# Rotary stage of a two-layer hybrid backbone: rotated result written to the tile of the rotated half and stored from there, context columns stored on their own

## Chip, cores, metric

The kernel runs as one program on one core of a Trainium2 chip. The metric is device microseconds (us) of one execution. A TensorE clock of 1.00 in the rows is 2.4 GHz, 0.50 is 1.2 GHz, and values between are a mix of the two over a stretch.

## The reference, cut to what matters

Two layers (l = 0, 1) run over 256 context tokens and 1024 latent tokens of width 1024. Each layer modulates the stream, applies one projection, splits its columns over three branches (a bidirectional RWKV-7 scan A, grouped-query attention B, neighbourhood attention C), gates them, projects back and normalises. The context is dropped after layer 0, so layer 1 needs no context queries.

The stage of this document prepares q and k of branch B. Each head is divided by its root mean square; latent tokens (not context tokens) are then rotated by position:

```python
def _apply_axial_rope(x, cos, sin):
    x1, x2, x3, x4 = jnp.split(x, 4, axis=-1)
    rotated = jnp.concatenate([-x2, x1, -x4, x3], axis=-1)
    return (x * cos[:, None] + rotated * sin[:, None]).astype(x.dtype)
...
gk_l = _apply_axial_rope(gk_l, cos, sin)
gq_l = _apply_axial_rope(gqa_q(aq_l), cos, sin)
gk_c, gv_c = gqa_kv(ak_c, av_c)
```

## The kernel before

Features lie on the 128 partitions, tokens on the columns: 256 context columns (`TC`), then 1024 latent ones (`TL`), 1280 in all (`T`). A feature block of 128 rows is one projection tile. Float32 products are split into high and low parts, three matmuls per 128 features (lines 203 to 205), into PSUM tiles of pool `pj` (3 buffers).

`layer_proj` runs the projections of a layer in order: RWKV inputs, two gate blocks, then four calls of `qk_proj` (k of both kv heads, then three q blocks of two heads each), the value projection (lines 415 to 417, matmuls into `pv`), and further on RWKV, the remaining projections and the attention.

`qk_proj` takes the PSUM blocks with ScalarE twice: squared into `sq` (line 347) and scaled into `raw` (line 348; the tile's name is `qr`). TensorE sums the squares (353), ScalarE and VectorE make the reciprocal root (354, 355), VectorE multiplies it into `raw` (356). Four DMAs copy the latent columns of `raw` with 32-partition groups swapped into `rot` (364); GpSimd multiplies `rot` by the sine and `raw` by the cosine (365, 366), VectorE adds (367), and one DMA stores to DRAM (368). `raw`, `sq` and `rot` each have two buffers. A new tile may be written only when everything that used the old tile in that buffer, DMAs included, has finished. For context columns `lo` is 0; in layer 1 only k has them, q calls have `lo` = 256.

All five engines run their own queue in order, and SyncE (SP) issues nearly all DMAs. The order within a queue is not the order of the code: a scheduler places each instruction by a simulated timeline when the kernel is built. So an edit in one stage can move instructions of others. This matters most in the stage in which the RWKV chain (waves of 4 steps; 40 steps per layer; line 724 is one product of each step, line 684 a merge, 713 and 734 the other products of the chain) and the attention (scores `st` of lines 963 and 964, running maximum 894 and 896, weighted values `y` 948) of a layer share the engines. They do not depend on each other; attention that is not done when the chain ends runs on alone.

Of the kernel before, what the change touches and what calls it, by code (L numbers as in the profile page):

```python
# [11 lines left out]
ALU = mybir.AluOpType  # L12
# [6 lines left out]
TC = 256  # L19
# [24 lines left out]
def body(tc, a):  # L44
    nc = tc.nc
# [136 lines left out]
    def layer_proj(l, hd, fw, lay, mid):  # L182
# [25 lines left out]
        def proj(m, evac, blocks=(0, 1, 2)):  # L208
            w = load_w(m)
            for b in blocks:  # L210
                block(w, b, evac)
# [58 lines left out]
        for c in range(3):  # L270
# [43 lines left out]
            for g in range(3):  # L314
                tts = range(4 * g, min(4 * g + 4, 10))
                pt = pq.tile([128, 4, 128], F32, tag="pq", name="pt")
                for j, tt in enumerate(tts):
# [6 lines left out]
                                  in_=vt[:, :n, :])  # L324
# [15 lines left out]
        def qk_proj(m, gcol, e, sc, dst, blocks):  # L340
            raw = sp.tile([128, T], F32, tag="qr", name="qr")
            sq = sp.tile([128, T], F32, tag="sq", name="sq")
            lo = 0 if 0 in blocks else TC

            def ev(b, ps):
                t0, n = BLK[b]
                nc.scalar.activation(out=sq[:, t0:t0 + n], in_=ps, func=AF.Square)
                nc.scalar.activation(out=raw[:, t0:t0 + n], in_=ps, func=AF.Copy, scale=gcol)  # L348
            proj(m, ev, blocks)
            for b in blocks:  # L350
                t0, n = BLK[b]
                ps = pq.tile([128, 512], F32, tag="pq", name="psn")
                nc.tensor.matmul(out=ps[:, :n], lhsT=bones, rhs=sq[:, t0:t0 + n], start=True, stop=True)
                nc.scalar.activation(out=sq[:, t0:t0 + n], in_=ps[:, :n], func=AF.Sqrt, scale=sc, bias=eps[:, e:e + 1])
            nc.vector.reciprocal(sq[:, lo:], sq[:, lo:])
            nc.vector.tensor_tensor(out=raw[:, lo:], in0=raw[:, lo:], in1=sq[:, lo:], op=ALU.mult)
            if not rope:
                for nm in ("cos", "sin"):
                    rope.append(sp.tile([128, TL], F32, tag=nm, name=nm, bufs=1))
                    nc.sync.dma_start(out=rope[-1], in_=a[nm])  # L360
            cos, sin = rope
            rot = sp.tile([128, TL], F32, tag="rot", name="rot")
            for q in range(4):
                nc.sync.dma_start(out=rot[32 * q:32 * q + 32, :], in_=raw[32 * (q ^ 1):32 * (q ^ 1) + 32, TC:T])
            nc.gpsimd.tensor_tensor(out=rot, in0=rot, in1=sin, op=ALU.mult)
            nc.gpsimd.tensor_tensor(out=raw[:, TC:], in0=raw[:, TC:], in1=cos, op=ALU.mult)
            nc.vector.tensor_tensor(out=raw[:, TC:], in0=raw[:, TC:], in1=rot, op=ALU.add)
            nc.sync.dma_start(out=dst[:, lo:], in_=raw[:, lo:])

        def store(dst, b, o):  # L370

# [26 lines left out]
        for i, m in list(enumerate(M_RG))[:2]:  # L398
            g_proj(m, gate_d[i], blks)
        qk_proj(M_AK, pp[:, l, PC_KN:PC_KN + 1], 1, 1.0 / 64, pair(k_d, 0), allb)  # L400
        qk_proj(M_AQ[0], pp[:, l, PC_QN:PC_QN + 1], 0, 1.0, pair(q_d, 0), blks)
        wvh = sp.tile([128, KT, 384], F32R, tag="wvh", name="wvh", bufs=1)
        wvl = sp.tile([128, KT, 384], F32R, tag="wvl", name="wvl", bufs=1)
# [5 lines left out]
        for i in (1, 2):  # L409
            qk_proj(M_AQ[i], pp[:, l, PC_QN:PC_QN + 1], 0, 1.0, pair(q_d, i), blks)  # L410
# [1018 lines left out]
```

## Time and profile before

| quantity | value |
|---|---|
| median of 3 runs | 2448.75 us (2443.36 to 2449.61) |
| profiled execution's own time | 2449.5 us |
| its span, first to last instruction | 2447.7 us |
| mean granted TensorE clock | 0.934 |
| busy: TensorE, VectorE, GpSimd, ScalarE | 90%, 66%, 48%, 41% |

In the rows below PE is TensorE, PEld its weight load, DVE VectorE, ACT ScalarE, POOL GpSimd, SP SyncE; PEq, SPq and so on are their queues. Matmuls overlap, so their starts tell the pace better than their durations do. An instruction with "[4.78 <-ACT qr L348]" behind it found its engine idle for 4.78 us before it, and the wait ended with that instruction. Line numbers are those of the kernel before; in the changed kernel what follows line 364 stands 2 lines later.

### The profile page before, as it was taken

To read this page: it belongs to the slowest core of one execution; us is meant where nothing else is said; L and a number is where in the kernel's file an instruction comes from. 1 tells how busy PE (TensorE), PEld (TensorE's weight loads), DVE (VectorE), ACT (ScalarE), POOL (GpSimd) and SP (SyncE) were. 2 spreads that over 40 slices of the span, in tenths; PEclk is the share of its full clock that TensorE was granted. 3 is DMA by queue.
4 is the path that set the end of the run, shared out by engine and by line. 5 is a ranking of instruction groups with operands and counts; after the bars stand their busy time and mean duration, and the time that the engine had idled before them with its cause. 6 is when DMAs were issued, how large, how long until landed. Compare 5 with 4: busy or idle time off the path is not lost. (4 is left out here: it accounts for less than half of the span.)

```text
span 2447.7 us, 57800 instructions
## 1 busy us (share of the span) xinstructions
PE 2206.0 (90%) x22616; PEld 1657.5 (68%) x22616; DVE 1615.7 (66%) x3063; ACT 1005.5 (41%) x2186; POOL 1180.5 (48%) x1438
## 2 busy tenths in 40 slices
PE   6999999997887898989999999899969888889897
PEld 3777898775555555555798777697746555556497
DVE  5687434445766878686387797524557788788746
ACT  3333413334544544454343443313345555545522
POOL 3465425424555555454155465533455565565453
PEclk9999999996887999989899999999968999999999
DMA  7344424527445544452233445335464545333342
GB/s 282 111 156 157 134 85 103 144 79 164 111 115 118 122 102 124 125 168 64 73 94 106 136 162 181 112 90 127 113 152 113 117 116 124 81 84 87 100 153 87
DMA packets 448241, 298.17 MB, mean 122 GB/s; under 512 B 249600, under 2 KB 395880, under 8 KB 446944
## 3 DMA queue, kind: packets, MB, share of 16 engines
q1 hardware_dynamic: 439936, 281.71, 41.9%
q0 software_dynamic: 7392, 10.28, 1.6%
q8 instruction: 178, 2.92, 0.5%
q10 hardware_dynamic: 640, 2.49, 0.4%
q14 instruction: 95, 0.78, 0.1%
HBM read 198.37 MB, written 91.79 MB: 119 GB/s over the span
## 5 line engine op out<-in xcount | busy, mean ns | idle before, releaser
L204 PE MATMUL pj<-hlo,wh 128*128 128x512 f32 (+1 forms) x1072 | 402.8, 376 | 13.1 <-DVE hlo L480 7.6
L203 PE MATMUL pj<-hhi,wh 128*128 128x512 f32 (+1 forms) x1072 | 403.2, 378 | 9.2 <-ACT qr L348 5.1
L205 PE MATMUL pj<-hhi,wl 128*128 128x512 f32 (+1 forms) x1072 | 402.0, 376 | 0.2 <-POOL wl L169 0.2
L204 PEld LDWEIGHTS pj<-hlo,wh 128*128 128x128 f32 x1072 | 205.7, 192 | 55.6 <-DVE hlo L480 7.7
L203 PEld LDWEIGHTS pj<-hhi,wh 128*128 128x128 f32 x1072 | 204.8, 192 | 54.3 <-issue 6.8
L169 POOL TENSOR_TENSOR wl<-wf,wh 128x512 fp32r<-128x512 f32 x104 | 142.9, 1379 | 202.7 <-ACT wh L168 185.4
L205 PEld LDWEIGHTS pj<-hhi,wl 128*128 128x128 f32 x1072 | 205.9, 192 | 38.6 <-issue 3.6
L896 DVE TENSOR_REDUCE mx<-sm 128x1 f32<-128x512 f32 (+1 forms) x372 | 199.1, 553 | 46.0 <-PE sm L894 43.7
L948 PE MATMUL y<-pt,v 128*64 128x256 f32 (+1 forms) x1392 | 214.0, 405 | 3.3 <-ACT pt L973 2.4
L970 ACT ACTIVATE pt<-st 128x512 f32<-128x512 f32 (+1 forms) x292 | 163.6, 583 | 129.5 <-PE st L964 125.7
L894 PE MATMUL sm<-k,q 128*128 128x256 f32 (+2 forms) x436 | 167.1, 429 | 34.6 <-DVE mx L896 26.8
L963 PE MATMUL st<-q,k 128*128 128x512 f32 (+3 forms) x376 | 165.9, 445 | 12.5 <-issue 3.5
L1197 PE MATMUL pj<-yl,wh 128*128 128x256 f32 x576 | 165.0, 289 | 2.0 <-POOL yl L1170 2.0
L1196 PE MATMUL pj<-yh,wh 128*128 128x256 f32 x576 | 162.8, 291 | 4.0 <-ACT wh L1147 2.1
L1198 PE MATMUL pj<-yh,wl 128*128 128x256 f32 x576 | 163.2, 288 | 0.1
L977 POOL TENSOR_TENSOR acc<-acc,pt 128x512 f32<-128x512 f32 x80 | 105.4, 1317 | 115.3 <-ACT pt L970 114.4
L948 PEld LDWEIGHTS y<-pt,v 128*64 128x64 f32 x1392 | 94.4, 144 | 90.8 <-issue 60.0
L894 PEld LDWEIGHTS sm<-k,q 128*128 128x128 f32 x436 | 82.8, 208 | 104.6 <-DVE mx L896 42.4
L964 PE MATMUL st<-q,k 65*128 65x512 f32 (+3 forms) x376 | 147.1, 395 | 0.6 <-ACT q L908 0.6
L625 DVE TENSOR_TENSOR G<-gt,msk 64x192 f32<-64x192 f32 (+1 forms) x320 | 110.5, 345 | 43.1 <-PE gt L620 32.0
L708 POOL MEMSET X<- 32x192 f32 x320 | 81.7, 255 | 89.1 <-PE py L754 59.9
L977 DVE TENSOR_TENSOR acc<-acc,pt 128x512 f32<-128x512 f32 x112 | 101.7, 918 | 30.3 <-ACT pt L970 29.8
(276 smaller groups left out, 5113.8 us busy)
## 6 DMA issues: line engine op xcount, KB each, us to landing
wf<-win SPq DMA_DIRECT2D x104, 256.0 KB
wm<-wmod SPq DMA_DIRECT2D x32, 512.0 KB
yf<-yg_d SPq DMA_DIRECT2D x72, 128.0 KB
wt<-wm SPq DMA_DIRECT2D x8, 1024.0 KB
gate_d<-o SPq DMA_DIRECT2D x32, 256.0 KB
wf<-wout SPq DMA_DIRECT2D x16, 512.0 KB
ldkk<-rw_d SPq DMA_DIRECT2D x40, 192.0 KB
ldkd<-rw_d SPq DMA_DIRECT2D x40, 192.0 KB
```

Source lines behind the costliest of these rows:

```text
L203: nc.tensor.matmul(out=ps[:, :n], lhsT=wh, rhs=hhi[:, k, t0:t0 + n], start=(k == 0), stop=False)
L204: nc.tensor.matmul(out=ps[:, :n], lhsT=wh, rhs=hlo[:, k, t0:t0 + n], start=False, stop=False)
L205: nc.tensor.matmul(out=ps[:, :n], lhsT=wl, rhs=hhi[:, k, t0:t0 + n], start=False, stop=(k == KT - 1))
L894: nc.tensor.matmul(out=sp_[:, :o], lhsT=q[0][:, qc:qc + 128], rhs=k[0][:, c0:c0 + o], start=True, stop=True)
L896: nc.vector.tensor_reduce(out=mx[:, n_:n_ + 1], in_=sp_[:, :o], op=ALU.max, axis=AX.X)
L948: mm = nc.tensor.matmul(out=y[64 * i:64 * i + 64, a0:a1], lhsT=v[:, t, :], rhs=pt[:, p0:p0 + a1 - a0], start=start, stop=stop and at == le ...
L963: nc.tensor.matmul(out=o, lhsT=k[0][:, 128 * t:128 * t + 128], rhs=q[0][:, qa:qb], start=True, stop=False)
L970: nc.scalar.activation(out=pt[:, :w], in_=sp_[:, :w], func=AF.Exp)
L977: eng.tensor_tensor(out=acc[i][:, :w], in0=sums[i][:, :w], in1=pt[:, :w], op=ALU.add)
L1196: nc.tensor.matmul(out=p_, lhsT=wh[m][:, k], rhs=yh, start=(x_ == 0), stop=False)
L1197: nc.tensor.matmul(out=p_, lhsT=wh[m][:, k], rhs=yl, start=False, stop=False)
L1198: nc.tensor.matmul(out=p_, lhsT=wl[m][:, k], rhs=yh, start=False, stop=(x_ == KT - 1))
```

## The change

The sum goes into `rot` instead of `raw`, and the store of the latent columns reads `rot`. Where context columns exist, they are stored from `raw` by a DMA of their own, issued behind the four swap DMAs. In layer 0 this makes two stores for each of the four calls, in layer 1 two for k and one for each q.

```diff
@@ -362,10 +362,12 @@
             rot = sp.tile([128, TL], F32, tag="rot", name="rot")
             for q in range(4):
                 nc.sync.dma_start(out=rot[32 * q:32 * q + 32, :], in_=raw[32 * (q ^ 1):32 * (q ^ 1) + 32, TC:T])
+            if not lo:
+                nc.sync.dma_start(out=dst[:, :TC], in_=raw[:, :TC])
             nc.gpsimd.tensor_tensor(out=rot, in0=rot, in1=sin, op=ALU.mult)
             nc.gpsimd.tensor_tensor(out=raw[:, TC:], in0=raw[:, TC:], in1=cos, op=ALU.mult)
-            nc.vector.tensor_tensor(out=raw[:, TC:], in0=raw[:, TC:], in1=rot, op=ALU.add)
-            nc.sync.dma_start(out=dst[:, lo:], in_=raw[:, lo:])
+            nc.vector.tensor_tensor(out=rot, in0=raw[:, TC:], in1=rot, op=ALU.add)
+            nc.sync.dma_start(out=dst[:, TC:], in_=rot)
 
         def store(dst, b, o):
```

SyncE's queue in the rotary stage of layer 1, before (`k_d` and `q_d` are the DRAM tensors of k and q, `ov` the values):

```order
L364 DMA rot_16871<-qr_16761 32x1024 x4
L368 DMA k_d_94<-qr_16761 128x1280
L364 DMA rot_16956<-qr_16880 32x1024 x4
L368 DMA q_d_93<-qr_16880 128x1024
L364 DMA rot_17075<-qr_16999 32x1024 x4
L420 DMA vg_d_95<-ov_17194 128x128
```

The same place in the changed kernel:

```order
L364 DMA rot_16875<-qr_16765 32x1024 x4
L366 DMA k_d_94<-qr_16765 128x256
L370 DMA k_d_94<-rot_16875 128x1024
L364 DMA rot_16961<-qr_16885 32x1024 x4
L370 DMA q_d_93<-rot_16961 128x1024
L364 DMA rot_17080<-qr_17004 32x1024 x4
L422 DMA vg_d_95<-ov_17199 128x128
```

The store of k is split, its larger part reads the `rot` tile, and nothing else has moved here. The fourth call's swap DMAs, not shown, stand behind the third value tile's first store in the changed kernel, and around the third q store before.

Of TensorE's queue in layer 0's shared stage, the rows before the merge in one step of the chain, before (`st` scores, `y` weighted values, `sm` running maximum, `ch` the chain):

```order
L963 MATMUL st_10529<-q1_10142,k1_10136 128x384
L964 MATMUL st_10529<-q2_10143,k21_9979 128x384
L948 MATMUL y_10455<-pt0_10501,v_10147 64x256
L948 MATMUL y_10455<-pt1_10508,v_10147 64x256
L894 MATMUL sm_10663<-k1_10435,q1_10441 128x384
L894 MATMUL sm_10666<-k1_10435,q1_10441 128x256
L963 MATMUL st_10543<-q1_10142,k1_10136 128x384
L964 MATMUL st_10543<-q2_10143,k21_9979 128x384
L724 MATMUL ch_2941<-rsb_5569,tt_4774 32x64 x12
```

The same step in the changed kernel:

```order
L965 MATMUL st_10547<-q1_10146,k1_10140 128x384
L966 MATMUL st_10547<-q2_10147,k21_9983 128x384
L965 MATMUL st_10554<-q1_10146,k1_10140 128x384
L966 MATMUL st_10554<-q2_10147,k21_9983 128x384
L950 MATMUL y_10459<-pt0_10529,v_10151 64x256
L726 MATMUL ch_2945<-rsb_5639,tt_4778 32x64 x12
L622 MATMUL gt_5354<-G5_2957,kb_5323 64x128 x6
L622 MATMUL gt_5365<-G5_2957,kb_5323 64x128 x6
L950 MATMUL y_10459<-pt1_10536,v_10151 64x256
L965 MATMUL st_10565<-q1_10146,k1_10140 128x384
L966 MATMUL st_10565<-q2_10147,k21_9983 128x384
```

The changed piece begins with the score product with which the former one ends (`st_10547` is the former `st_10543`) and holds two more, one ahead of the chain's product and one ahead of the merge: attention stands further ahead of the chain. Counted over TensorE's whole queue, the score products of line 963 that stand ahead of the product of line 724 in the 16th, 22nd and 40th (last) step of layer 0's chain are 34, 58 and 140 of 208 before, and 36, 68 and 145 in the changed kernel. In layer 1 these counts agree to within 2, with smaller moves within steps.

## Rows read from the trace of the kernel before

**Rows 1.** The page's first part: busy time, share of the span and instructions of each engine.

```profile
PE 2206.0 (90%) x22616; PEld 1657.5 (68%) x22616; DVE 1615.7 (66%) x3063; ACT 1005.5 (41%) x2186; POOL 1180.5 (48%) x1438
```

**Rows 2.** TensorE's waits in layer 1's rotary stage (1536 to 1612 us): in total, times, longest.

```profile
PE pj L203 <- ACT qr L348: 4.8, 1, 4.8
```

**Rows 3.** The chain of work that ended last, 1564 to 1572 us: start, us, what.

```profile
1564.86 2.30 DVE qr L367
1567.17 3.04 DMA k_d<-qr
1570.45 0.70 ACT qr L348
1571.19 0.80 PE pj L203
```

**Rows 4.** ScalarE's timeline at that place: start, us, instruction, idle before it and what ended it.

```profile
1559.98 0.69 ACT L354 ACTIVATE sq<-psn,eps 128x512 f32<-128x512 f32 x1 [0.26 <-PE psn L353]
1570.45 1.27 ACT L348 ACTIVATE qr<-pj,pp 128x512 f32<-128x512 f32 x2 [9.78 <-DMA k_d<-qr]
```

**Rows 5.** TensorE's timeline there, the matmuls around the wait.

```profile
1566.01 0.40 PE L205 MATMUL pj<-hhi,wl 128*128 128x512 f32 x1
1571.19 0.80 PE L203 MATMUL pj<-hhi,wh 128*128 128x512 f32 x1 [4.78 <-ACT qr L348]
1571.78 0.63 PE L204 MATMUL pj<-hlo,wh 128*128 128x512 f32 x1
...
1576.47 0.53 PE L203 MATMUL pj<-hhi,wh 128*128 128x512 f32 x1
1576.85 0.40 PE L204 MATMUL pj<-hlo,wh 128*128 128x512 f32 x1
...
1579.19 0.40 PE L205 MATMUL pj<-hhi,wl 128*128 128x512 f32 x1
```

**Rows 6.** The same timeline earlier, around a shorter wait.

```profile
1545.12 1.12 PE L353 MATMUL psn<-sq,c_bones 128*128 128x512 f32 x2 [1.17 <-ACT sq L347]
...
1546.78 0.40 PE L203 MATMUL pj<-hhi,wh 128*128 128x512 f32 x1
1547.02 0.39 PE L204 MATMUL pj<-hlo,wh 128*128 128x512 f32 x1
```

**Rows 7.** Busy time by stretch: PE, PEld, DVE, ACT and POOL busy us (instructions), then granted clock, DMA share and GB/s.

```profile
1571.00:1577.00 6.00, 5.81 (x14) 4.61 (x15) 4.67 (x1) 1.78 (x4) 3.74 (x2) 0.52 0.15 34
1577.00:1592.00 15.00, 14.70 (x75) 12.90 (x74) 10.76 (x5) 3.98 (x7) 5.72 (x3) 1.00 0.30 88
```

**Rows 8.** SyncE's queue in layer 1's rotary stage: start, us of issuing, DMAs.

```profile
1554.91 2.51 SPq L364 DMA_DIRECT2D rot<-qr  x4
1567.17 0.34 SPq L368 DMA_DIRECT2D k_d<-qr  x1
1568.31 2.42 SPq L364 DMA_DIRECT2D rot<-qr  x4
...
1581.22 3.49 SPq L364 DMA_DIRECT2D rot<-qr  x4
```

**Rows 9.** Busy time by stretch as in rows 7: layer 0 in and behind its rotary stage, layer 1 behind it.

```profile
300.00:350.00 50.00, 49.86 (x268) 46.65 (x269) 22.48 (x7) 9.81 (x20) 14.27 (x6) 1.00 0.33 97
...
1600.00:1650.00 50.00, 50.00 (x266) 45.92 (x265) 9.77 (x14) 8.70 (x17) 19.56 (x36) 1.00 0.27 73
1650.00:1700.00 50.00, 50.00 (x393) 39.55 (x393) 21.72 (x72) 18.05 (x44) 19.82 (x25) 1.00 0.59 140
```

**Rows 10.** TensorE's waits in layer 0's rotary stage (250 to 345 us).

```profile
PE pj L203 <- ACT qr L348: 0.3, 1, 0.3
```

**Rows 11.** Busy time by stretch as in rows 7: layer 0's shared stage and the attention that follows alone.

```profile
560.00:700.00 140.00, 115.93 (x1891) 81.73 (x1887) 99.04 (x289) 64.69 (x160) 71.67 (x97) 0.77 0.54 124
700.00:800.00 100.00, 80.78 (x1118) 54.38 (x1116) 62.83 (x184) 46.23 (x121) 49.27 (x76) 0.76 0.53 120
800.00:900.00 100.00, 87.74 (x1552) 57.56 (x1549) 85.35 (x218) 46.98 (x122) 52.17 (x78) 0.97 0.47 111
900.00:1000.00 100.00, 88.98 (x1392) 56.30 (x1393) 73.63 (x168) 52.15 (x128) 55.97 (x71) 0.91 0.47 119
1000.00:1065.00 65.00, 63.50 (x877) 39.71 (x877) 48.66 (x100) 35.76 (x85) 30.55 (x35) 0.95 0.39 107
1065.00:1200.00 135.00, 122.53 (x725) 70.82 (x723) 86.98 (x153) 61.97 (x120) 54.50 (x42) 0.89 0.32 97
```

**Rows 12.** Line 963 alone (score products) by stretch: PE busy, PEld busy, clock, DMA share, GB/s.

```profile
700.00:800.00 100.00, 9.68 (x23) 4.91 (x23) 0.76 0.53 120
...
1000.00:1065.00 65.00, 10.36 (x24) 4.50 (x24) 0.95 0.39 107
1065.00:1200.00 135.00, 30.85 (x68) 13.88 (x68) 0.89 0.32 97
```

**Rows 13.** Line 724 alone (24 recorded matmuls are one step of the chain) by stretch, columns as in rows 12.

```profile
700.00:800.00 100.00, 3.88 (x144) 2.75 (x144) 0.76 0.53 120
800.00:900.00 100.00, 3.90 (x168) 2.78 (x168) 0.97 0.47 111
900.00:1000.00 100.00, 3.24 (x144) 2.28 (x144) 0.91 0.47 119
1000.00:1065.00 65.00, 3.55 (x144) 2.50 (x144) 0.95 0.39 107
```

## The prediction

> **What bounds the kernel.** I read the busy times first: TensorE is busy for 90% of the span, its weight load for 68% and no other engine for more than 66% [rows 1]. So a wait elsewhere counts only where it makes TensorE idle or lets its clock fall. Then the waits of TensorE in the two rotary stages, since the change is there. In layer 0 the tile `qr` costs TensorE 0.3 us [rows 10], and the stretch from 300 to 350 us is full, 49.86 of 50 [rows 9]. In layer 1 the same wait costs 4.8 us, once [rows 2]. The chain of waits says what stands behind it: VectorE's sum of k (1564.86, 2.30 us), then k's store (1567.17, 3.04 us to landing), then ScalarE's line 348 at 1570.45, then TensorE at 1571.19 [rows 3]. ScalarE agrees: it had been idle 9.78 us for that store [rows 4]. This is the third call's `qr`, which takes the buffer that k's `qr` had; the store is the last that reads it. Last, the stages where the order moves: the shared stage of layer 0 by stretches, with its score products and its steps [rows 11 to 13].
>
> **The wait that goes.** In the changed kernel `qr` is free when the sum has read it, at 1564.86 + 2.30 = 1567.16 instead of 1570.45: 3.29 us earlier, I take 3.3. The context store also reads `qr`, but it stands right behind swap DMAs issued from 1554.91 for 2.51 us [rows 8]; if it takes as long to land as the five times larger store, 3.04 us, and starts at 1557.5, it ends by 1560.6, before the sum. So the sum becomes the last reader, and TensorE still idles about 4.78 - 3.3 = 1.5 us: what is late next is VectorE's sum. Bounds: 0 if something else is as late as the store, 3.3 if nothing is. ScalarE's queue shows nothing between 1559.98 and 1570.45 [rows 4], so I take the upper end.
>
> **The clock behind it.** After the 4.78 us pause TensorE ran at 0.52 for 6 us and at 1.00 after that [rows 7]. From the matmul at 1571.19 to the one at 1576.85 lie 13 intervals between starts, 5.66 us; from there to 1579.19 lie ten, 2.34 us, 0.234 us each [rows 5]. Thirteen at that pace are 3.04 us, so the low clock cost 2.6 us. A pause of 1.17 us before had no such effect: the matmuls behind it start 0.24 us apart [rows 6]. The pause that is left, 1.5 us, is nearer to 1.17 than to 4.78, so I count the whole 2.6 us as regained; bounds 0 and 2.6. Sum for layer 1: 3.3 + 2.6 = 5.9 us. It reaches the end if TensorE stays the limit behind it, and it does: 50.00 of 50 us from 1600 to 1650 and again to 1700 [rows 9].
>
> **What is added.** Five context stores, four in layer 0 and one in layer 1, at an issue of 0.34 us each (k's store [rows 8]); the store they come from shrinks from 1280 to 1024 columns. SyncE has idle time around all of them, and TensorE's full stretches cover it [rows 9]: nothing. In layer 0, and in layer 1, the fourth call's swap DMAs move behind a value tile's store, so GpSimd's products and the last q store come some 3 us later; the value products on TensorE cover that too, and nobody reads q before the attention. If that cover were gone it would cost these 3 us once per layer.
>
> `rot` is now held until its own store has landed. k's `rot` is stored from 1567.17; the buffer is next filled at 1581.22 [rows 8], 14.05 us later, and a store took 3.04 us [rows 3]. So there are 11 us of slack and the cost is nothing. The Trainium skill speaks against the move here ("DMA: Bandwidth & Descriptors", section "Anatomy of one DMA"): each DMA has a fixed part of about 2.0 us, mostly the wait for its write to complete, above all when it goes to HBM, so a tile that a store reads is held long past its last byte. By its formula 512 KB would be held an estimated 3.2 us; the trace shows 3.04 us for 640 KB, and by either figure the slack remains.
>
> **The order of layer 0.** The scheduler places more attention beside the chain: 32 score products instead of 24 from the 16th to the 22nd step, five more in all when the chain ends. The trace has 68 of line 963 behind the chain [rows 12], as the order says (208 - 140). They take 135 us [rows 11], 1.99 us each with all that hangs on them, so five fewer shorten the attention that runs alone by 9.9 us. What do they cost earlier? Behind 800 us stand 19 steps of 40 [rows 13], so the 22nd falls near 800 us, and the eight extra products land mostly between 700 and 800 us, where TensorE is busy 80.78 of 100 us at clock 0.76 [rows 11]. There 23 products stand beside 6 steps in 100 us, while from 1000 to 1065 us 24 products and 6 steps took 65 us [rows 12, 13]. Room is there, so the low end of the cost is 0. The high end is that the five cost there what they cost later, 9.9 us. I take the middle: 5.0 us stay. The waits of the new order itself no row can give; they are the rivals below. Layer 1 has nearly the same order, and I put its small moves at 0.
>
> Sum, against the profiled execution's own 2449.5 us: 2449.5 - 3.3 - 2.6 - 5.0 = 2438.6 us, so 10.9 us or 0.44% less. The median of the runs is 2448.75, 0.75 us lower, within their spread.
>
> **Rivals.** First, only layer 1 gains: the eight products displace as much as they save. For it: VectorE is at 85 of 100 us from 800 to 900 [rows 11], so attention pulled forward may wait there. 2449.5 - 5.9 = 2443.6 us.
>
> Second, a slower kernel: more attention ahead of the chain holds the chain back, because TensorE, VectorE and ScalarE work in order and a chain product behind a score waits with it. The place is layer 0 behind the 22nd step. From 800 to 1065 us 19 steps run in 265 us, 13.9 us each, and from 700 to 800 a step takes 16.7 us [rows 13]. If these 19 went half of the way to that slow pace, 1.4 us each, 26.6 us are lost; with 5.9 and 9.9 us gained the net is 10.8 us: 2460.3 us. It decides from (7.3 + 15.8) / 19 = 1.2 us per step, 7.3 us being 0.3% of the time. Against it: the steps from 1000 to 1065 us carry as many scores at 10.8 us each.
>
> Third, the opposite: the added attention fills the slow stretch and keeps the clock up, and its 6 steps go half of the way from 16.7 to 10.8 us, 17.7 us. With 5.9 and 9.9: 2416.0 us. For it the clock of 0.76; against it, that the waits there are the chain's own.
>
> Fourth, the change does not do what it says: line 348 is held by something else that ends as late as the store, and the order breaks even. 2449.5 us. Rows 4 speak against it.
>
> **Chances and range.** The forecast with its own range, 2433.7 (the order costs nothing) to 2443.6 (it costs all it saves) has 0.40; the first rival 0.22, the second 0.18, the third 0.12, the fourth 0.08. A difference under 0.3%, about 7.3 us, can't be told from no change. The forecast lies beyond it in four fifths of its range: 0.32 + 0.12 and 0.02 from the first rival make faster 0.46; the rest of the forecast, most of the first and the fourth make same 0.36; the second slower 0.18. The range reaches from a third of the way to the third rival's full price, 2422, to the slower rival, 2460.
>
> **What would show it.** In the changed profile, ScalarE's line 348 of layer 1's third call should be released by VectorE's sum (now line 369), not by a store; TensorE's pause there should be about 1.5 us, with no clock of 0.5 behind it. In layer 0 some 63 score products should stand behind the chain, and that stretch should be about 10 us shorter; the 16th to the 22nd step should take no longer than before. If layer 1's rotary stage ends less than 3 us earlier, my first term is wrong; if the steps of layer 0 behind the 22nd take over 1.2 us more each, the slower rival holds.

## The result

The changed kernel takes 2429.84 us, the kernel before 2448.65 us on the same chip (medians of 20 runs each): a ratio of 0.9925, 95% interval 0.9907 to 0.9943; the medians lie 18.8 us apart. Its profiled execution took 2434.79 us, with a span of 2432.7 us. One of the 20 executions of the changed kernel took 10802.86 us, for a reason that is not known; the ratio leaves it out. The others scatter from 2410 to 2445 us, those of the kernel before from 2438 to 2454 us, so a few us in a single trace prove little; the runs below are read as groups.

The busy line of the page, as in [rows 1]:

```profile
PE 2187.5 (90%) x22616; PEld 1644.4 (68%) x22616; DVE 1611.0 (66%) x3063; ACT 1007.1 (41%) x2186; POOL 1179.8 (48%) x1438
```

TensorE executes the same 22616 instructions in 18.5 us less busy time, at a mean granted clock of 0.937 instead of 0.934. That more of them ran at the full clock is read below from the stretches.

**Layer 1's rotary stage.** TensorE's wait [rows 2], the chain [rows 3], ScalarE [rows 4], TensorE [rows 5] and SyncE [rows 8] at the same place in the changed kernel:

```profile
PE pj L203 <- ACT qr L348: 1.6, 1, 1.6
```

```profile
1542.69 2.39 POOL qr L368
...
1545.10 2.31 DVE rot L369
...
1547.43 0.70 ACT qr L348
...
1548.17 0.50 PE pj L203
```

```profile
1547.43 1.27 ACT L348 ACTIVATE qr<-pj,pp 128x512 f32<-128x512 f32 x2 [6.56 <-DVE rot L369]
```

```profile
1548.17 0.50 PE L203 MATMUL pj<-hhi,wh 128*128 128x512 f32 x1 [1.56 <-ACT qr L348]
1548.51 0.40 PE L204 MATMUL pj<-hlo,wh 128*128 128x512 f32 x1
1548.74 0.40 PE L205 MATMUL pj<-hhi,wl 128*128 128x512 f32 x1
```

```profile
1537.56 0.59 SPq L366 DMA_DIRECT2D k_d<-qr  x1
1547.42 0.33 SPq L370 DMA_DIRECT2D k_d<-rot  x1
...
1560.08 3.32 SPq L364 DMA_DIRECT2D rot<-qr  x4
```

The store has left the chain: ScalarE starts in the same moment as the store is issued, not after it has landed. TensorE idles 1.56 us instead of 4.78, and the matmuls behind it start 0.23 us apart, the pace of the full clock. The context store is issued 9.9 us before the sum ends and holds nobody up.

**Layer 0's shared stage.** The stretches of [rows 11], with the last one begun at the start of the chain's last step and ended where the output projection goes on behind the attention (this stretch is called the tail from here on), and line 965 alone (the former 963) as in [rows 12]:

```profile
560.00:700.00 140.00, 114.65 (x1769) 80.10 (x1769) 97.23 (x281) 65.47 (x160) 76.36 (x99) 0.79 0.53 119
700.00:800.00 100.00, 87.49 (x1259) 56.31 (x1259) 77.78 (x221) 56.46 (x143) 58.40 (x84) 0.93 0.63 145
800.00:900.00 100.00, 83.30 (x1470) 55.27 (x1469) 77.93 (x206) 43.16 (x110) 48.97 (x75) 0.90 0.45 104
900.00:1000.00 100.00, 86.03 (x1399) 54.21 (x1397) 69.60 (x158) 50.54 (x130) 48.83 (x66) 0.88 0.47 118
1055.20:1183.17 127.97, 114.76 (x760) 67.29 (x759) 85.44 (x144) 62.77 (x123) 56.43 (x42) 0.93 0.32 98
```

```profile
700.00:800.00 100.00, 12.39 (x34) 6.41 (x34) 0.93 0.63 145
...
1056.00:1183.00 127.00, 27.58 (x63) 12.51 (x62) 0.93 0.32 99
```

The row to look at is the second. From 700 to 800 us TensorE does 34 score products instead of 23, beside the same six steps of the chain. It is busy 6.7 us more, but its clock is 0.93 instead of 0.76. The steps themselves got shorter there. The 16th and the 22nd step start, before and then after, with these rows:

```profile
710.54 0.86 PE L724 MATMUL ch<-rsb,tt 32*32 32x64 f32 x24
810.83 0.54 PE L724 MATMUL ch<-rsb,tt 32*32 32x64 f32 x24
```

```profile
714.63 0.54 PE L726 MATMUL ch<-rsb,tt 32*32 32x64 f32 x24
804.30 0.54 PE L726 MATMUL ch<-rsb,tt 32*32 32x64 f32 x24
```

That is 89.7 us from the 16th to the 22nd instead of 100.3. The steps ahead of the 16th and behind the 22nd gave it back: behind the 22nd it is 250.9 us instead of 244.4, some 0.4 us more for each step. The last step starts at 1055.20 us, before at 1055.27. As the first score product started 2.9 us earlier in the changed kernel, that makes 486.8 us instead of 484.0. Behind the chain stand 63 score products as counted, and the output projection goes on behind the attention at 1183.17 instead of 1198.72 us.

The whole of layer 0 from the first score product to the start of the last output-projection product, before and then after, columns as in [rows 7]:

```profile
571.25:1314.08 742.83, 665.51 (x8170) 466.39 (x8170) 537.50 (x1185) 339.99 (x797) 360.71 (x452) 0.89 0.44 113
```

```profile
568.38:1298.46 730.08, 649.03 (x8146) 455.68 (x8146) 533.12 (x1182) 339.26 (x796) 360.60 (x451) 0.91 0.45 115
```

TensorE idles 742.83 - 665.51 = 77.3 us before and 730.08 - 649.03 = 81.1 us after: the extra attention has not filled idle time on balance. The busy time is 16.5 us shorter, at a clock of 0.91 instead of 0.89. Busy time times clock is 592 us before and 591 us after: the same work, done at a higher clock. So the 12.8 us of layer 0 are the clock's.

### The profile page after: what moved, and what is told of

It is laid out like the page before. It is cut to its first block, busy times and chain, and to the rows that moved or that the text cites. A ratio compares the mean times of both kernels' runs of the same rounds, so it can differ in the third digit from the quotient of the medians.

```text
span 2432.7 us, 57804 instructions
## 1 busy us (share of the span) xinstructions
PE 2187.5 (90%) x22616; PEld 1644.4 (68%) x22616; DVE 1611.0 (66%) x3063; ACT 1007.1 (41%) x2186; POOL 1179.8 (48%) x1438
```

## The experiments

Twelve kernels ran, each beside runs of the kernel before on its chip. The table gathers what the trace of each shows: score products ahead of the 22nd and of the last chain step of layer 0 (by the order of the queue), the clock from 700 to 800 us, the start of layer 0's last chain step, and three spans: layer 0 as above, layer 1's rotary stage (first reciprocal of a q or k call to the last value product), and layer 1 from its first score product to the start of its last output-projection product. All are differences of starts, in us. Where attention stands between the products of one step (e7, e9, e10), the counts go up to its last product.

| kernel | ratio and interval | 22nd, last | clock | chain's end | layer 0 | rotary | layer 1 |
|---|---|---|---|---|---|---|---|
| before | 1 | 58, 140 | 0.76 | 1055 | 742.8 | 81.0 | 623.7 |
| changed | 0.9925 (0.9907 to 0.9943) | 68, 145 | 0.93 | 1055 | 730.1 | 75.3 | 633.8 |
| e1, early store holds | 0.9935 (0.9907 to 0.9963) | 68, 145 | 0.93 | 1064 | 729.8 | 77.1 | 630.6 |
| e2, third buffer | 0.9903 (0.9872 to 0.9935) | 68, 145 | 0.95 | 1059 | 725.3 | 73.3 | 618.3 |
| e3, layer 1 only | 1.0012 (0.9993 to 1.0031) | 58, 140 | 0.76 | 1059 | 744.4 | 73.8 | 633.6 |
| e4, layer 0 only | 1.0044 (1.0026 to 1.0062) | 68, 145 | 0.95 | 1057 | 727.6 | 81.5 | 657.3 |
| e5, late store holds | 0.9947 (0.9919 to 0.9974) | 68, 145 | 0.90 | 1062 | 733.0 | 83.7 | 628.3 |
| e6, split only | 0.9984 (0.9965 to 1.0003) | 61, 134 | 0.83 | 1052 | 739.7 | 79.3 | 631.2 |
| e7, offset 3000 | 1.0126 (1.0097 to 1.0154) | 68, 158 | 0.86 | 1082 | 730.1 | 74.4 | 685.5 |
| e8, offset 4000 | 1.0268 (1.0238 to 1.0298) | 68, 208 | 0.95 | 1162 | 752.5 | 74.3 | 690.2 |
| e9, before at 2800 | 1.0035 (1.0012 to 1.0058) | 58, 145 | 0.79 | 1072 | 748.9 | 79.6 | 630.1 |
| e10, early, 40 rounds | 1.0020 (0.9995 to 1.0045) | 81, 169 | 0.90 | 1086 | 723.0 | 74.2 | 650.9 |
| e11, early, 36 rounds | 0.9950 (0.9930 to 0.9971) | 72, 162 | 0.85 | 1093 | 740.1 | 75.6 | 630.2 |
| e12, early, 25 rounds | 0.9952 (0.9934 to 0.9971) | 70, 146 | 0.86 | 1053 | 722.2 | 75.2 | 636.6 |

**e1: a store that holds `qr` again.** The changed kernel and a spare store of layer 1's `qr`:

```diff
             nc.sync.dma_start(out=dst[:, TC:], in_=rot)
+            if l:
+                nc.sync.dma_start(out=hold_d, in_=raw[:, TC:])
```

> The changed kernel with one more DMA in layer 1 only: each call also stores the latent columns of the qr tile to a spare DRAM tensor, behind the store of rot, so that qr is again held until a store has landed. The order on all engines is otherwise that of the changed kernel. Theory (the release of qr in layer 1 is worth about 5.9 us: 3.3 of pause and 2.6 of low clock, the rest of the gain is the order of layer 0): 5 to 6 us slower than the changed kernel, so some 12 us faster than before (ratio about 0.995); TensorE's pause in front of line 203 in layer 1's rotary stage back at about 4.8 us, with a clock near 0.5 behind it. Rival (the wait was hidden anyway, and all of the gain is order): same as the changed kernel, ratio 0.9925.

The spare store needs only GpSimd's product, not the sum, so it was issued beside the sum, and the pause became 1.98 us instead of 4.8. As a test of the wait it is a miss. But TensorE's timeline around the pause shows something:

```profile
1551.54 0.50 PE L204 MATMUL pj<-hhi,wh 128*128 128x512 f32 x1 [1.98 <-ACT qr L349]
...
1552.57 0.55 PE L205 MATMUL pj<-hlo,wh 128*128 128x512 f32 x1
1552.92 0.63 PE L206 MATMUL pj<-hhi,wl 128*128 128x512 f32 x1
1553.34 0.63 PE L204 MATMUL pj<-hhi,wh 128*128 128x512 f32 x1
...
1555.90 0.47 PE L204 MATMUL pj<-hhi,wh 128*128 128x512 f32 x1
```

The matmuls first start 0.23 us apart, then from 1552.92 to 1555.90 us 0.43 us apart, the pace of the 1.2 GHz level. A pause of 1.98 us was followed by a low clock, one of 1.56 us in the changed kernel was not. The length alone does not decide it, as the last section shows.

**e5: the hold made to wait for the sum.**

```diff
             nc.sync.dma_start(out=dst[:, TC:], in_=rot)
+            if l and not lo:
+                nc.vector.tensor_copy(raw[:, TC:TC + 8], rot[:, 0:8])
+                nc.sync.dma_start(out=hold_d, in_=raw[:, TC:])
```

> The changed kernel, but in layer 1's k call VectorE copies 8 columns of the sum back into the qr tile behind the sum, and a spare store to DRAM reads the latent columns of that tile (1024 columns, issued behind the store of rot). So a store that waits for the sum holds the buffer again, in layer 1 alone; layer 0 keeps the changed kernel's order. Theory (the wait is worth what was counted): TensorE's pause at the third call comes back to 4.5 to 5.5 us with a clock near 0.5 for some 6 us behind it, the rotary stage from the first reciprocal to the last value product is about 81 us instead of 75.3, and the time lies 5 to 7 us above the changed kernel's, a ratio of 0.995. Rival (the order of layer 0 is everything, and what the rotary stage gains is given back later): pause back, but the ratio stays at 0.9925.

The spare store was issued behind a swap DMA of the next call, so the pause grew to 7.17 us, more than the 4.5 to 5.5 expected, with the clock at 0.50 behind it (TensorE's timeline, then the busy time of the 6 us behind the pause):

```profile
1563.36 0.80 PE L204 MATMUL pj<-hhi,wh 128*128 128x512 f32 x1 [7.17 <-ACT qr L349]
```

```profile
1563.40:1569.40 6.00, 6.00 (x14) 4.74 (x15) 2.12 (x2) 0.97 (x2) 4.70 (x2) 0.50 0.00 0
```

By the prediction's own terms this pause should cost 7.17 - 1.56 + 2.6 = 8.2 us against the changed kernel. The rotary stage took 83.7 us instead of 75.3, 8.4 us more. The ratio is 0.0022 above the changed kernel's, 5.4 us, as the theory had it; but the two intervals overlap, so the whole time alone would not prove it.

**e2: only the buffer.** The kernel before with a third buffer for `qr`; sum and store as before:

```diff
-            raw = sp.tile([128, T], F32, tag="qr", name="qr")
+            raw = sp.tile([128, T], F32, tag="qr", name="qr", bufs=3)
```

> The kernel before with a third buffer for the qr tile and nothing else: the sum still goes into qr, one store. TensorE's and GpSimd's orders come out as those of the changed kernel, row for row. Theory (what matters is only that qr's next user need not wait for the store, on the chip and in the scheduler's timeline): as fast as the changed kernel, ratio 0.9925, within 5 us. With a third buffer not even the sum has to be waited for, so the pause of TensorE in layer 1 should be under 1 us. Rival (it is the smaller store, or the sum's destination): no gain, ratio 1.00.

It gains as much as the change, and TensorE shows no wait for `qr` at all. Its TensorE queue is the changed kernel's, row for row. So the change works through the release of `qr`, and through nothing else that it edits: the scheduler of the build sees the earlier release too, and that is what rearranged layer 0. The busy time from 700 to 800 us is like the changed kernel's:

```profile
700.00:800.00 100.00, 88.06 (x1317) 56.70 (x1306) 78.99 (x221) 56.35 (x143) 59.52 (x85) 0.95 0.62 145
```

**e3 and e4: the change in one layer only.** `L` is 1 in e3 and 0 in e4; the other layer keeps the former sum and store:

```diff
+            if not lo and l == L:
+                nc.sync.dma_start(out=dst[:, :TC], in_=raw[:, :TC])
...
+            if l == L:
+                nc.vector.tensor_tensor(out=rot, in0=raw[:, TC:], in1=rot, op=ALU.add)
+                nc.sync.dma_start(out=dst[:, TC:], in_=rot)
+            else:
+                nc.vector.tensor_tensor(out=raw[:, TC:], in0=raw[:, TC:], in1=rot, op=ALU.add)
+                nc.sync.dma_start(out=dst[:, lo:], in_=raw[:, lo:])
```

> The change in layer 1 alone; layer 0 has the code and the order of the kernel before (score products ahead of the last chain step: 140 of 208). Theory: only the 5.9 us of layer 1's rotary stage, ratio about 0.9976, the end of layer 0's chain and the 143 us behind it as before; layer 1's shared stage has a slightly different order (142 ahead of its last step instead of 143), worth within 5 us. Rival (the order of layer 0 gives nothing, the gain comes from layer 1): the whole 18 us here.

> The change in layer 0 alone. Layer 0's order is that of the changed kernel (145 of 208 ahead of the last step); layer 1's rotary stage keeps the wait for the store, and in layer 1 the scheduler now puts only 130 of 168 score products ahead of the last chain step instead of 143. Theory: layer 0's attention behind the chain 15 us shorter as in the changed kernel; layer 1's pause 4.8 us; 13 more products behind layer 1's chain, at 2.0 us each 26 us longer there unless the chain ends earlier for it. If the chain ends where it did: about 11 us slower than before; if it ends as much earlier as it is relieved: 15 us faster. Rival (counts of products behind the chain don't set the time): layer 1 as long as before although 13 more stand behind its chain.

The stage readings separate as they should. In e3 the wait is 1.4 us and the rotary stage 7.2 us shorter, while layer 0 is that of before. Its stretch from 700 to 800 us:

```profile
700.00:800.00 100.00, 79.81 (x1129) 53.46 (x1128) 64.97 (x190) 47.74 (x123) 50.31 (x77) 0.76 0.53 121
```

In e4 layer 0 is that of the changed kernel, and the wait of 4.8 us is back in layer 1:

```profile
700.00:800.00 100.00, 89.10 (x1381) 57.06 (x1381) 78.18 (x222) 57.49 (x146) 58.06 (x85) 0.95 0.61 143
```

```profile
PE pj L203 <- ACT qr L348: 4.8, 1, 4.8
```

Yet neither is faster in the end. Half of the change moves layer 1's order, which the whole change leaves as it was: e3 has 36 instead of 28 score products ahead of the 16th step and 142 instead of 143 of 168 at the end, e4 has 130 at the end, so 38 instead of 25 behind the chain. In e4 layer 1 took 657.3 us against 623.7, which alone is more than what layer 0 gained. In e3 it took 633.6; one trace cannot tell that from the scatter, since kernels with the changed kernel's counts in layer 1 took 618 to 634 us. But the 7.2 us by which e3's rotary stage is shorter do not show in its whole time (ratio 1.0012, where 0.9976 was expected). So the two halves cannot be added up; the order of a later stage is part of the price of any edit here.

**e6: the split alone.**

```diff
+            if not lo:
+                nc.sync.dma_start(out=dst[:, :TC], in_=raw[:, :TC])
...
-            nc.sync.dma_start(out=dst[:, lo:], in_=raw[:, lo:])
+            nc.sync.dma_start(out=dst[:, TC:], in_=raw[:, TC:])
```

> The kernel before with the store of k and q split into context and latent columns, the sum still written to qr and stored from there. In this order 134 of 208 score products stand ahead of layer 0's last chain step, so 74 stand behind it (68 before, 63 in the changed kernel). Theory (the buffer, not the split, makes the gain; products behind the chain set layer 0's end at about 2 us each): pause of 4 to 5 us in layer 1 as before, layer 0 from its last chain step to its first output projection about 155 us against 143.5 before, ratio 1.003 to 1.006. Rival (the split store is what helps, it lands sooner): pause under 3.5 us and a ratio below 0.998.

The wait is 3.9 us, the whole no different from before: the split is not what gains. But the theory's figure for layer 0 missed. With 74 score products behind the chain the tail took 143.6 us, not 155, as long as the 143.5 us of before with 68. About 2 us for each score product is no law of the tail; what else is left of the attention, and the clock (0.92 in this tail, 0.88 before), count as much.

**e7 and e8: still more attention ahead of the chain.**

```diff
-        attention(l)
+        with tc.high_priority(offset=3000):
+            attention(l)
```

(4000 in e8.)

> The changed kernel with the attention built under a higher priority of the scheduler (offset 3000), so that 158 instead of 145 of 208 score products stand ahead of layer 0's last chain step and 168 instead of 143 of 168 ahead of layer 1's; up to the 28th step of layer 0 the counts are the same. Theory (what stands behind the chain sets the end, the chain has room for it): layer 0's tail falls from 128 to about 102 us, at 2 us for each of 13 products, layer 1's tail too, and the chain's ends move by less than half of that: ratio 0.97 to 0.98. Rival (TensorE has no room left, every product placed earlier costs there what it costs later): tails shorter but the chains end as much later, ratio 0.990 to 0.995. Second rival (the chain is held back by more than is saved): ratio above 1.0.

> The same with offset 4000: all 208 score products of layer 0 stand ahead of the last chain step (116 by the 28th, 170 by the 34th), all 168 of layer 1 too (126 by the 28th). Theory: layer 0's tail loses most of its 128 us, but the last 12 steps must now carry 92 score products more than the 22 to 28 us for 3 steps that the rows show, so the chain ends 60 to 130 us later; ratio 0.96 to 1.0, and whether it is below the run at 3000 says from where the chain pays in full. Rival (chain held back): ratio above 1.01.

Both are slower, and my theory fell. In e7 the 13 additional products stand late, behind the 28th step; there the clock is high already (0.94 and 0.92 in e7 from 800 to 900 and to 1000 us), and they cost what they save: the chain ends 27 us later, and layer 0 as a whole takes the 730.1 us of the changed kernel. Layer 1, with all of its score products ahead of the chain's end, takes 52 us longer. This is the second rival of the prediction, the chain held back, in an order that goes further than the change. In e8 layer 0 pays too: its chain ends 107 us later, and the layer takes 22 us longer; layer 1 takes 56 us longer.

**e9: as many behind the chain, but not placed early.** The kernel before, only the scheduler's priority of layer 0's attention changed:

```diff
-        attention(l)
+        with tc.high_priority(offset=2800 if l == 0 else 1):
+            attention(l)
```

> The kernel before (nothing of the change in it) with the attention of layer 0 built under a priority offset of 2800, which gives 34, 58, 82, 116 and 145 of 208 score products ahead of the 16th, 22nd, 28th, 34th and last chain step: as many behind the chain as in the changed kernel (63), but between the 16th and the 22nd step still the 24 of before, not 32. In the runs so far layer 0 took from its first score product to its last output projection 743 and 747 us with the order of before and 725 to 733 us in the five kernels with the changed order, and the clock from 700 to 800 us was 0.76 in the first and 0.90 to 0.95 in the second. Theory (the gain is the clock, kept up by the attention placed between the 16th and the 22nd step): clock from 700 to 800 us 0.74 to 0.82, layer 0 738 to 747 us, ratio 0.997 to 1.003, since layer 1's wait is still there. Rival (only the number behind the chain counts): layer 0 725 to 733 us, ratio 0.992 to 0.995.

(By the starts of the table, layer 0 of e3 took 744 us, not the 747 of that text.) The stretch from 700 to 800 us, and the tail:

```profile
700.00:800.00 100.00, 84.19 (x1183) 56.76 (x1175) 66.78 (x184) 50.03 (x131) 52.57 (x78) 0.79 0.57 132
...
1073.20:1200.70 127.50, 116.28 (x740) 68.90 (x739) 86.48 (x144) 62.12 (x121) 56.22 (x42) 0.92 0.31 98
```

Counted from the chain's last product, the tail is as short as the changed kernel's, 127.5 us, with the same 63 products. But the chain ends 16 us later, and layer 0 takes 749 us, a little beyond what I expected and far from the rival's 725 to 733. The clock from 700 to 800 us stays low. So it isn't the number behind the chain that gains. That the products must stand where TensorE's clock is low fits this run, but the run does not show it alone.

**e10 to e12: the first rounds of layer 0's attention earlier still.** The changed kernel, with the body of the attention's loop in

```diff
+            with tc.high_priority(offset=N if l == 0 and n_it < K else 1):
```

where `n_it` counts rounds of two score products; N and K are 4500 and 40 in e10, 4500 and 36 in e11, 2800 and 25 in e12.

> The changed kernel with the first 40 rounds of layer 0's attention loop built under a priority offset of 4500 and the rest at 1: 48, 81, 112, 140 and 169 score products ahead of the 16th, 22nd, 28th, 34th and last step instead of 36, 68, 93, 120 and 145; 24 fewer behind the chain, and of those that move 12 lie ahead of the 16th and 19 ahead of the 28th step. Theory (attention placed where TensorE is at a low clock and idle between the chain's products costs little, attention placed late costs its full time, as offset 3000 showed with 730 us for layer 0): clock from 560 to 700 us above 0.85 instead of 0.79, layer 0 705 to 722 us instead of 730, ratio 0.980 to 0.990. Rival (the room was used up by the first eight): layer 0 725 to 735 us, ratio 0.990 to 0.995. Second rival (the chain is held back): layer 0 above 740 us, ratio above 0.997.

> As the run of the early attention, with the first 36 instead of 40 rounds under the offset of 4500: 48, 72, 104, 136 and 162 score products ahead of layer 0's five steps, and in layer 1 the same counts as the changed kernel (28, 52, 85, 113, 143; the run before had 137, and its layer 1 took 651 us from the first score product to the last output projection against 618 to 634 with the changed order). Theory (what that run lost lay in layer 1's order, its layer 0 gained 7 us): layer 0 718 to 727 us, layer 1 618 to 634 us, ratio 0.984 to 0.992, so at or a little below the changed kernel's 0.9925. Rival (attention ahead of the chain costs its full time in the next layer too, whatever the counts): layer 1 above 640 us, ratio above 0.996.

> The changed kernel with the first 25 rounds of layer 0's attention under an offset of 2800: 44, 70, 95, 120 and 146 score products ahead of the five steps (36, 68, 93, 120, 145 in the changed kernel), so eight products more by the 16th step and one more at the end. Theory (early attention is free while the clock is low): chain's end within 5 us of the changed kernel's 1055 to 1064, clock from 560 to 700 us above 0.80, layer 0 724 to 733 us, ratio 0.989 to 0.995. Rival (the chain is held back where attention moves ahead of it): chain's end above 1070 us, layer 0 above 738 us, ratio above 0.996.

e10 has the shorter layer 0, 723 us, but only by letting TensorE run nearly full behind 800 us, where the chain loses 31 us. Its layer 1, with another order, lost 17 us. The first and the third stretch of layer 0 in e10:

```profile
560.00:700.00 140.00, 118.96 (x1777) 81.64 (x1771) 102.88 (x295) 72.95 (x176) 78.67 (x101) 0.84 0.61 139
800.00:900.00 100.00, 96.16 (x1282) 60.78 (x1279) 77.81 (x185) 53.93 (x136) 62.63 (x78) 0.97 0.46 113
```

e11 got layer 1 back to 630 us as its theory said, but its layer 0 took 740 us, so it missed too. e12 is the cleanest of the three: by the counts, eight more products by the 16th step and nearly nothing else in layer 0.

```profile
560.00:700.00 140.00, 115.89 (x1909) 79.39 (x1908) 104.07 (x301) 71.80 (x175) 81.30 (x102) 0.86 0.62 139
700.00:800.00 100.00, 81.91 (x1238) 54.18 (x1227) 76.80 (x205) 46.81 (x122) 49.20 (x76) 0.86 0.55 123
```

The clock from 560 to 700 us rises from 0.79 to 0.86, though from 700 to 800 us it is 0.86 where the changed kernel had 0.93; the chain ends at 1053 us, and layer 0 takes 722.2 us, 8 us less than in the changed kernel and a little less than I expected. As a whole e12 is not faster than the changed kernel, though: in its trace layer 1's projections, from layer 0's last output product to the first rotary reciprocal, took 231.9 us against 224.0, and layer 1 636.6, with 81 instead of 85 score products ahead of its 28th step. Why is not settled. None of the tries beats the change; only the third buffer is as good.

## Why the prediction was right, and where its sum was not

The forecast was 2438.6 us, 10.9 us less than the profiled execution before; the median measured is 18.8 us lower than before. At 2429.84 us it lies below the forecast's own range, 2433.7 to 2443.6, and inside the whole one, 2422 to 2460. So the direction and the whole range held; the whole range held only because it reached towards the third rival. The terms:

- **The wait that goes: right.** ScalarE was released by the sum, and the pause left was 1.56 us where 1.5 was counted. The difference is 4.78 - 1.56 = 3.2 us, against 3.3.
- **The clock behind it: right in this case.** No low clock followed. Together the two were counted as 5.9 us; the rotary stage is 5.7 us shorter. Over the runs, the kernels with a wait of 3.9 to 4.8 us (before, e4, e6, e9) took 79.3 to 81.5 us, those with one of 0.9 to 1.8 us (changed, e3, e7, e8, e10 to e12) 73.8 to 75.6. That these us reach the kernel's end is not shown: e5 points to it, with overlapping intervals, and e3 does not.
- **What is added: right.** The context stores show up in no wait of TensorE. `rot` of k was stored from 1547.42 and refilled from 1560.08, 12.7 us later, and the store was in no chain there. The Trainium skill ("DMA: Bandwidth & Descriptors", section "Anatomy of one DMA") gives a fixed part of about 2.0 us for each DMA on the path that GpSimd issues on; these stores go out on SyncE's queue, where k's store took 3.04 us for 640 KB before [rows 3]. That the store holds `rot` until it has landed cost nothing here, for want of anybody who waited.
- **The order of layer 0: mis-sized.** "I take the middle: 5.0 us stay", with bounds from 0 to 9.9. The trace shows 12.8 us for layer 0. Over all runs, the two kernels with the order of before took 742.8 and 744.4 us (mean 743.6), the five with the changed order 725.3 to 733.0 (mean 729.2): 14.4 us. That is beyond the upper bound, because the clock of layer 0 stood in none of the sum's terms. It enters in two places.

The first is the tail. I priced each score product at 1.99 us "with all that hangs on them" and five of them at 9.9. Before, the tail was

```profile
1055.27:1198.72 143.45, 130.98 (x844) 76.31 (x843) 90.69 (x162) 67.19 (x135) 57.37 (x45) 0.88 0.31 95
```

143.45 us against 127.97 in the changed kernel, so it is 15.5 us shorter. (My 135 us for it began at 1065 us, some 10 us behind the chain's end.) Busy time times clock is 115 us before and 107 us in the changed kernel: 8 to 9 us of work left the tail, about what I counted. Most of the rest is its clock, 0.93 instead of 0.88, which I had not counted. Part of that may be scatter: the tail's clock was 0.88 and 0.90 in the two kernels with the order of before and 0.91 to 0.96 in the five with the changed one, but 0.92 in e6 and e9. TensorE's groups in that stretch, before (1056 to 1198.7 us) and after (1056 to 1183.1 us), in the columns line, engine, operation, names, shapes and count, then busy us and mean ns, then idle us before them:

```profile
L948 PE MATMUL y<-pt,v 128*64 128x256 f32 (+1 forms) x264 | 39.6, 417 | 0.0
L963 PE MATMUL st<-q,k 128*128 128x512 f32 (+1 forms) x68 | 30.8, 457 | 0.8 <-DVE am L110 0.8
L894 PE MATMUL sm<-k,q 128*128 128x512 f32 (+1 forms) x54 | 22.4, 452 | 8.5 <-DVE mx L896 8.5
L907 PE MATMUL mt<-c_ident,nm 128*1 128x128 f32 x56 | 9.6, 327 | 0.4 <-DVE mx L896 0.4
```

```profile
L950 PE MATMUL y<-pt,v 128*64 128x256 f32 (+1 forms) x248 | 36.1, 399 | 0.3 <-ACT pt L972 0.3
L965 PE MATMUL st<-q,k 128*128 128x512 f32 (+1 forms) x63 | 27.9, 445 | 0.2 <-DVE gtl L1027 0.2
L896 PE MATMUL sm<-k,q 128*128 128x512 f32 (+1 forms) x48 | 18.4, 405 | 4.3 <-DVE mx L898 4.3
L909 PE MATMUL mt<-c_ident,nm 128*1 128x128 f32 x36 | 6.6, 332 | 3.5 <-DVE mx L898 3.5
```

Score products and weighted values fell by about the share that I counted, 5 of 68. Of the running maximum's products 6 of 54 moved ahead of the chain, and of its transposes 20 of 56: larger shares, 7 us of busy time in all. The mean ns of the score products and of the running maximum's fell too, from 457 to 445 and from 452 to 405.

The second is the cost in between. I set its high end at what the tail gains and its low end at 0, and took half, 4.9 us. From the first score product to the chain's last step it was 2.8 us: 486.82 us instead of 484.02, with TensorE busy for the same 420 us, although more attention stood in it.

```profile
571.25:1055.27 484.02, 420.07 (x6417) 276.67 (x6416) 361.60 (x935) 236.22 (x592) 250.50 (x347) 0.87 0.49 117
```

```profile
568.38:1055.20 486.82, 420.65 (x6475) 276.05 (x6474) 361.10 (x948) 240.16 (x604) 253.79 (x349) 0.88 0.50 118
```

The reason is in the third rival, which I gave 0.12: the added attention kept the clock up. Its other half, faster steps, came in part: the 16th to the 22nd took 10.6 us less, where the rival had 17.7, but the other steps gave it back. With 15.5 - 2.8 = 12.7 us for layer 0 instead of 5.0, the sum would have been 5.9 + 12.7 = 18.6 us, against 18.8 between the medians. That they agree so closely is in part luck, since single traces scatter by more.

- **Layer 1's order "at 0": not a loss that the runs show.** In this trace layer 1 took 10 us more than before, but e2, with the same TensorE order, took 618.3 us. That is scatter between executions.
- **The rivals.** "Only layer 1 gains" is refuted by e4 and by the layer 0 column. "The change does not do what it says" fell with the release by the sum. "A slower kernel, the chain held back" did not happen here, as the steps behind the 22nd took 0.4 us more each, not 1.2; but e7 and e9 show that it begins close by: 13 and 5 products placed late suffice.

What stays open: that a filled TensorE kept its clock, rather than something else in the new order, rests on ten kernels in two groups and on e12. The seven whose TensorE queue up to 800 us is the changed kernel's (itself, e1, e2, e4, e5, e7, e8) had 0.86 to 0.95 from 700 to 800 us; the three with the order of before there, or nearly (before, e3, e9), 0.76 to 0.79. e6, with 61 score products ahead of the 22nd step, lies between at 0.83. The two orders, and that of e12, differ in other rows as well. A kernel that adds useless work in that stretch and leaves every order alone was not tried, since the scheduler moves the order with any added instruction.

## What to carry to other kernels

Write a result to the tile whose buffer is needed last, or give the contended tile one more buffer: a store then leaves the path, and the gain is the wait plus the low clock behind it. Where a scheduler places instructions, look at what the release does to the order of far stages, since here that was the larger part; and price moved work by the clock of the stretch that it moves into: placed at 0.76 it cost about 3 us where the tail lost 15.5, placed late at 0.9 and above it cost its full time or more (e7, e9). Look at the clock of the stretch that the work leaves, too. Count every kind of instruction that leaves a tail, not the one that is easiest to count.

## What the runs showed of the hardware

The length of a single TensorE pause did not settle whether the clock fell. A pause of 1.98 us was followed by some 3 us at 1.2 GHz (e1), pauses of 1.56 us (the changed kernel) and 1.78 us (e11) by none. But one of 1.97 us in e9 was followed by none either, and a pause in front of the transposes of line 319 in layer 1 was 2.56 us long both before and in e9, with the full clock behind it in the one and a low one in the other. TensorE's timeline and the busy time of the 4 us behind the pause, before and then in e9:

```profile
1509.69 1.31 PE L319 MATMUL pt<-c_ident,v 128*128 128x128 f32 x10 [2.56 <-DVE v L230]
1509.69:1513.69 4.00, 4.00 (x21) 3.16 (x22) 3.92 (x4) 1.70 (x3) 3.92 (x3) 1.00 0.35 131
```

```profile
1507.21 2.33 PE L319 MATMUL pt<-c_ident,v 128*128 128x128 f32 x10 [2.56 <-DVE v L230]
1507.21:1511.21 4.00, 4.00 (x14) 3.06 (x15) 3.89 (x4) 1.17 (x2) 3.92 (x3) 0.57 0.35 131
```

I had argued from 1.17 and 4.78 us and overlooked this pause of 2.56 us in the same trace. The seven kernels with a pause of 0.9 to 1.8 us at the third call had no low clock behind it, but with a little more than the 1.5 us that I counted, the 2.6 us of the clock might not have come back whole.

The stretch from 700 to 800 us ran at a granted clock of 0.76 before and of 0.93 in the changed kernel, with TensorE busy 81 and 87 of 100 us: the page's busy share hides most of such a difference, the clock beside it shows it.
